# Uneven placement of the seven-product units in the mixer's weave

## The chip, the cores and the metric

The kernel runs on one core of a Trainium2 chip. The metric is the device time of one execution in microseconds (us). The kernel before takes 2188.45 us, the median of three runs that lie between 2188.09 and 2190.01 us.

## The reference

One encoder layer on x of 256 rows by 2048 columns, all in float32: a SwiGLU block with a norm, a mixer with a norm, a second SwiGLU block with a norm, and a gated per-layer embedding. The change touches the mixer:

```python
proj = x @ w_in
mq, mk, mv, mo, mi, mf, sq, sk, sv, ga, gb = _split_cols(proj)
...
y_m = (h.reshape(bsz, s, D_M) * jax.nn.sigmoid(mo)).astype(x.dtype)
y_sb = _stick_breaking(_heads(sq, N_HEADS_SB), _heads(sk, N_HEADS_SB), _heads(sv, N_HEADS_SB))
merged = jax.nn.sigmoid(ga) * (y_m @ w_up_m) + jax.nn.sigmoid(gb) * (y_sb @ w_up_sb)
return merged @ w_out
```

`h` is the output of a chunkwise mLSTM with 4 heads of 256; `y_sb` is stick-breaking attention with 8 heads of 128. `ga` and `gb` have 2048 columns each, `mo` has 1024.

## The kernel before

**Matmuls.** Each float32 operand is split into a high part that TensorE takes in its float32r format and a low part, the rest. A product needs three matmuls (L1259 to L1261: high by high, high by low, low by high). A *unit* (class `Unit`) is one weight tile of 256 rows by up to 512 columns, against one half of the 256 tokens: two steps of 128 rows, so six matmuls of up to 512 columns. A weight tile is loaded by DMA as `raw` (L1182, 512 KB), ScalarE casts its high half (L1210, `split`), VectorE subtracts to get the low half (L1214). `splits_due` keeps tiles split ahead of TensorE: the mode "wide" that holds during the weave allows 8 raw tiles and 6 split ones.

**Plain groups.** `group` makes pairs of units: one weight tile is used for both token halves. A pair therefore needs one split for two units.

**Seven-product units.** `seven` computes two column groups for two token halves as a two-by-two block product with seven products instead of eight (`both7` calls it for two column groups of `w_in`). It makes 28 units: four of product 1, four of product 2, then four rounds of products 5, 7, 6, 4, 3. Every unit has a weight tile of its own, and four of the seven tiles are sums of others, which VectorE makes with an addition in place (L361, `raw<-raw`). The finished products are combined by VectorE (L396 in `put`, L402 in `rest`) or copied by ScalarE (L412). Within the four rounds five PSUM banks stay in use at a time, beside the two of the plain group that runs at the same time; there are eight.

**Order.** All engines' instructions are written out in one pass over `program`, a list of units. Small steps of the attention branches (`mlstm`, `gated`, `stick`, `sb_turn`) are generators in a scheduler, `Sched`, whose clock goes on by 6 x 0.2161 us for each full unit; a step is written out when its due time on that clock has come, and each engine then runs its own instructions in the order written. PSUM tiles, `mm` for units and `ms` for small steps, share the eight banks. The matmuls of the small steps stand among those of the units: L705 (transposes after a projection), L867 and L881 (mLSTM), L916 (transposes of the gated mLSTM output, whose low half VectorE makes in L922), L935 (scores of stick-breaking attention), L948 and L949 (cumulative sums, which VectorE takes from PSUM in L950), L959 (attention by values). L833 and L944 are VectorE steps of the same attention.

**The weave.** In the mixer a stretch of the program mixes two lists (L1061 to L1063). `main` has 144 units in plain groups:

- `sb(10, 11, 4, 5)`, `sb(20, 21, 22, 23)`, `sb(12, 13, 6, 7)`: 16 units each; `sb(14, 15)`: 16 units with 256 columns only. They give the stick-breaking heads their inputs, and the chains of attention steps run beside them and beside the gate groups.
- `branch(0, 0)` and `branch(0, 1)`: 16 units each, the gates of column group 0. ScalarE takes their sigmoid straight from PSUM.
- `ups(0, True)`, `ups(1)`, `ups(2)`: 16 units each, the products with `w_up_m` and `w_up_sb`. VectorE multiplies each with its gate (L1019, L1021). Before `ups(0)` the mLSTM outputs that were written to DRAM are read back (`bring_ym_back`).

`side` has 4 x 28 seven-product units: the output gate `mo`, which the gated mLSTM steps wait for, then `pair(1)`, `pair(2)`, `pair(3)`, the gates of column groups 1 to 3, which `ups(1)`, `ups(2)` and, behind the weave, `ups(3)` need. `weave` puts side units behind main units, at an even rate.

Of the kernel before, what the change touches and what calls it, by code (L numbers as in the profile page):

```python
# [23 lines left out]
COL = 512  # L24
# [80 lines left out]
class ActT:  # L105
# [17 lines left out]
    def ready(self, c, tt):  # L123
        return self.left.get((c, tt)) == 0
# [35 lines left out]
        self.name = name  # L160


def weave(main, side):

    n = sum(isinstance(u, Unit) for u in main)
    out, at, seen = [], 0, 0
    for u in main:
        out.append(u)
        if isinstance(u, Unit):
            seen += 1  # L170
            while at < len(side) and at * n < seen * len(side):
                out.append(side[at])
                at += 1
    return out
# [11 lines left out]
def kernel(  # L186
# [9 lines left out]
    w_in, w_out, w_up_m, w_up_sb = w_in[0], w_out[0], w_up_m[0], w_up_sb[0]  # L196
# [194 lines left out]
    def both7(w, ca, cb, act, dest, ready, loaded):  # L391

        r, held = {}, {}

        def put(k, t, a, b, op):
            nc.vector.tensor_tensor(out=r[k, t], in0=a, in1=b, op=op)  # L396

        def rest():
            u = r[0, 1]
            put(0, 1, held[7], u, ALU.add)  # L400
            z = r[1, 1] = dest(1, 1)
            nc.vector.scalar_tensor_tensor(out=z, in0=u, scalar=-1.0, in1=held[5],  # L402
                                           op0=ALU.mult, op1=ALU.subtract)
            ready(1, 1)
            return
            yield

        def done(m, ps):
            held[m] = ps
            if m == 1:  # L410
                r[0, 1] = dest(0, 1)
                nc.scalar.copy(r[0, 1], ps)  # L412
            elif m == 2:
                r[0, 0] = dest(0, 0)
                put(0, 0, ps, r[0, 1], ALU.add)
                ready(0, 0)
            elif m == 6:
                r[1, 0] = dest(1, 0)
                put(0, 1, ps, r[0, 1], ALU.add)
                put(1, 0, held[5], r[0, 1], ALU.add)  # L420
                sched.spawn(rest(), DELAY["rest"])
            elif m == 4:
                sched.until(lambda: (1, 1) in r)
                put(0, 1, ps, r[0, 1], ALU.add)
                ready(0, 1)
            elif m == 3:
                put(1, 0, ps, r[1, 0], ALU.subtract)
                ready(1, 0)

        return seven(w, ca, w, cb, D, COL, act, done, loaded)  # L430

    program = []

    def mode(name):
        program.append(Mode(name))
# [105 lines left out]
    def ffn(w1, w3, w2, act, norm, skew=True, ahead=()):  # L541
# [74 lines left out]
        def down(*chunks):  # L616
            pairs = []
            for g in range(D // COL):
                def add(ps, t, g=g):
# [11 lines left out]
                    + down(6, 8, 7))  # L631
        side = [u for c in (1, 2, 3, 5, 6, 7, 9, 10) for u in up7(c)]
        program.extend(main[:HEAD] + weave(main[HEAD:], side))
        program.append(norm.load)
        program.extend(ahead)
# [13 lines left out]
    x1T = ActT(act_tile, ActT(act_tile), True)  # L649
# [334 lines left out]
    def sb(*heads):  # L984
        if heads[0] >= 16:
            col0 = sq0 + heads[0] * DS
        else:
            col0 = [(sq0 + h * DS, 2 * DS) for h in heads[::2]]
        return flat(group(w_in, range(0, D, 2 * P), col0, len(heads) * DS, x1T,
                          lambda ps, t: sb_columns(ps, t, heads)))  # L990
# [40 lines left out]
    def branch(g, half):  # L1031
        return flat(group(w_in, range(0, D, 2 * P), ga0 + half * D + g * COL, COL, x1T, gate_done(g, half)))

    def ups(g, swap=False):
        parts = [flat(group(w_up_m, range(0, HM * DM, 2 * P), g * COL, COL, ymT, up_done(g, 0, swap))),
                 flat(group(w_up_sb, range(0, HS * DS, 2 * P), g * COL, COL, ysbT, up_done(g, 1, not swap)))]
        if swap:
            parts.reverse()
        return parts[0] + parts[1]

    def gate_dest(g):
        def dest(k, t):
            if (g, t) not in gt:
                gt[g, t] = big()
            return gt[g, t][:, k * COL:(k + 1) * COL]
        return dest

    def gate_ready(g):
        def sigmoid(k, t):
            a = gt[g, t][:, k * COL:(k + 1) * COL]  # L1050
            activate(a, a, ACT.Sigmoid)
            flags.add(("gate", g, t, k))
            return
            yield
        return lambda k, t: sched.spawn(sigmoid(k, t), DELAY["sig"])

    def pair(g):
        return both7(w_in, ga0 + g * COL, ga0 + D + g * COL, x1T, gate_dest(g), gate_ready(g), False)

    program.append(sticks)  # L1060
    main = sb(10, 11, 4, 5) + sb(20, 21, 22, 23) + sb(12, 13, 6, 7) + sb(14, 15) + branch(0, 0) + branch(0, 1) + [bring_ym_back] + ups(0, True) + ups(1) + ups(2)  # L1061
    mode("wide")
    program.extend(weave(main, both7(w_in, 3072, 3072 + COL, x1T, mo_dest, mo_ready, False) + pair(1) + pair(2) + pair(3)))  # L1063
    mode("mix")
    program.append(bring_back)
    program.append(lambda: [sched.spawn(merge_turn(g, t), 1.0 + 2.0 * g + t) for g in range(3) for t in range(TT)])
# [69 lines left out]
    at = len(program) - 24  # L1136
# [160 lines left out]
```

## Time and profile before

| | |
|---|---|
| Median of three runs | 2188.45 us |
| The profiled execution | 2189.97 us |
| Its span, first to last instruction | 2188.3 us |
| TensorE busy | 2175.6 us |
| VectorE busy | 1902.8 us |
| ScalarE busy | 1316.0 us |
| Mean DMA rate | 260 GB/s |

In rows of the profile PE is TensorE's matmuls, PEld its weight loads, DVE is VectorE, ACT is ScalarE, POOL is GpSimd, SP is SyncE, which issues the DMAs. A row of instructions of one line shows the line, engine, operation, output<-inputs, shapes and the count, then the busy time in us, the mean of one in ns and, behind the second bar, the idle time of the engine before them with what ended it. A row of the waits shows who waited for whom, with the total in us, the number of waits and the longest. A row of stretches shows its length and each engine's busy time with its count of instructions, then the granted TensorE clock, the DMA engines' share and GB/s. A row of the timeline has the start and the duration in us; where it ends in xN it joins N instructions in a row, and a bracket gives the idle time before it. TensorE's matmuls overlap, so their durations are longer than the time from one start to the next.

### The profile page before, as it was taken

How to read it: one execution, taken by the hardware profiler on the slowest of the kernel's cores; microseconds unless marked ns; L12 is line 12 of the kernel's file. 1: busy time of each engine (PE TensorE's matmuls, PEld its weight loads, DVE VectorE, ACT ScalarE, POOL GpSimd, SP SyncE). 2: the span in 40 equal slices, each digit the busy share in tenths (PEclk: the TensorE clock that was granted, in tenths of full speed). 3: DMA queues.
4: the chain of work that ended last, by engine and by line, in shares of the span. 5: the costliest groups of instructions: out<-in, count | busy, mean ns of one | idle time of the engine just before them, and what ended most of it. 6: DMA issues, size and time to landing. Idle time of an engine off the chain costs nothing.

```text
span 2188.3 us, 28264 instructions
## 1 busy us (share of the span) xinstructions
PE 2175.6 (99%) x9966; PEld 1800.1 (82%) x9966; DVE 1902.8 (87%) x2108; ACT 1316.0 (60%) x1591; POOL 97.9 (4%) x88
## 2 busy tenths in 40 slices
PE   9999999999999999999999999999999999999999
PEld 7888888888887888888888888888888888888888
DVE  6999999899998765898988985699999999999974
ACT  7555655556564755667775554566665555665572
POOL 0100000010000000000000000000010000000000
PEclk9999999999999999999999999999999999999999
DMA  9899999899994775667878886589999999999753
GB/s 336 249 306 283 289 295 305 273 279 315 308 333 155 214 233 154 193 206 209 299 217 281 271 267 212 183 236 309 287 275 305 306 272 290 309 295 321 253 166 102
DMA packets 302222, 568.52 MB, mean 260 GB/s; under 512 B 18264, under 2 KB 39680, under 8 KB 302080
## 3 DMA queue, kind: packets, MB, share of 16 engines
q1 hardware_dynamic: 280320, 524.77, 71.8%
q0 software_dynamic: 21760, 41.95, 11.2%
q8 instruction: 78, 1.28, 0.2%
q14 instruction: 64, 0.52, 0.1%
HBM read 560.35 MB, written 6.29 MB: 259 GB/s over the span
## 4 chain that ended last, share of the span: by engine, by line
PE 92%; DMA 3%; DVE 3%; issue 1%; ACT 1%; POOL 0%; SPq 0%; DVEq 0%; POOLq 0%; ACTq 0%
PE mm L1261 29%; PE mm L1259 29%; PE mm L1260 29%; DMA raw<-in_ffn_w_dram 3%; DVE split L1214 2%; PE ms L290 1%; PE ms L495 0%; ACT split L1210 0%; DVE big L621 0%; DVE raw L361 0%; PE ms L959 0%; DMA raw<-in_w_in_dram 0%; PE ms L867 0%; PE ms L881 0%; PE ms L935 0%
## 5 line engine op out<-in xcount | busy, mean ns | idle before, releaser
L1210 ACT CAST split<-raw 128x1024 fp32r<-128x1024 f32 (+2 forms) x1061 | 1060.7, 1037 | 522.5 <-PE mm L1260 150.7
L1214 DVE TENSOR_TENSOR split<-raw,split 128x1024 fp32r<-128x1024 f32 (+2 forms) x1061 | 1240.7, 1200 | 137.0 <-ACT split L1210 119.1
L1259 PE MATMUL mm<-split,actT 128*128 128x512 f32 (+2 forms) x3120 | 1216.7, 390 | 0.1
L1261 PE MATMUL mm<-split,actT 128*128 128x512 f32 (+2 forms) x3120 | 1203.0, 386 | 3.3 <-DVE actT L297 3.3
L1260 PE MATMUL mm<-split,actT 128*128 128x512 f32 (+2 forms) x3120 | 1202.0, 385 | 1.8 <-DVE split L1214 1.7
L1261 PEld LDWEIGHTS mm<-split,actT 128*128 128x128 f32 x3120 | 586.1, 188 | 124.5 <-DVE actT L297 5.4
L1260 PEld LDWEIGHTS mm<-split,actT 128*128 128x128 f32 x3120 | 586.8, 188 | 117.0 <-DVE split L1214 4.8
L1259 PEld LDWEIGHTS mm<-split,actT 128*128 128x128 f32 x3120 | 586.5, 188 | 114.1 <-issue 1.3
L361 DVE TENSOR_TENSOR raw<-raw 128x1024 f32<-128x1024 f32 x240 | 292.5, 1219 | 2.2
L1187 POOL DMA_DIRECT2D raw<-in_ffn_w_dram x80 | 95.4, 1193 | 1879.9 <-DVE temp L559 786.3
L292 ACT CAST actT<-ms 128x512 fp32r<-128x512 f32 x60 | 35.0, 586 | 76.9 <-PE ms L290 75.8
L568 DVE TENSOR_TENSOR temp<-mm,temp 128x512 f32<-128x512 f32 x112 | 76.8, 685 | 4.2 <-PE mm L1261 1.9
L621 DVE SCALAR_TENSOR_TENSOR big<-mm,big 128x512 f32<-128x512 f32 x96 | 65.1, 682 | 7.3 <-PE mm L1261 7.2
L297 DVE TENSOR_TENSOR actT<-ms,actT 128x512 fp32r<-128x512 f32 x60 | 40.7, 683 | 17.4 <-ACT big L296 9.0
L236 ACT ACT_TABLE_LOAD x35 | 44.9, 1283 | 0.6
L285 DVE TENSOR_TENSOR actT<-temp,actT 128x512 fp32r<-128x512 f32 x40 | 26.5, 687 | 17.3 <-ACT actT L284 17.1
L240 ACT ACTIVATE temp<-mm 128x512 f32<-128x512 f32 (+1 forms) x22 | 12.3, 559 | 44.8 <-PE mm L1261 44.8
L240 ACT ACTIVATE temp<-temp 128x512 f32<-128x512 f32 (+1 forms) x48 | 28.5, 595 | 9.9 <-DVE temp L568 7.3
L284 ACT CAST actT<-temp 128x512 fp32r<-128x512 f32 x40 | 24.1, 621 | 13.0 <-DVE temp L308 12.1
L240 ACT ACTIVATE rstd<-mv,eps 128x1 f32<-128x1 f32 x6 | 1.8, 295 | 45.1 <-DVE mv L478 45.1
L1076 DVE SCALAR_TENSOR_TENSOR big<-big,mm 128x512 f32<-128x512 f32 x8 | 5.5, 685 | 26.9 <-PE mm L1261 26.9
L794 DVE SCALAR_TENSOR_TENSOR temp<-ms,cw,temp 128x253 f32<-128x253 f32 (+2 forms) x48 | 22.4, 480 | 7.3 <-ACT temp L240 6.1
(128 smaller groups left out, 561.2 us busy)
## 6 DMA issues: line engine op xcount, KB each, us to landing
raw<-in_ffn_w_dram SPq DMA_DIRECT2D x655, 512.0 KB, 6.3
raw<-in_w_in_dram SPq DMA_DIRECT2D x176, 512.0 KB, 4.6
raw<-in_ffn_w_dram POOLq DMA_DIRECT2D x80, 512.0 KB, 9.2
raw<-in_w_out_dram SPq DMA_DIRECT2D x32, 512.0 KB, 6.0
raw<-in_w_in_dram SPq DMA_DIRECT2D x56, 256.0 KB, 3.7
raw<-in_w_ple_gate_dram SPq DMA_DIRECT2D x24, 512.0 KB, 4.6
raw<-in_w_up_sb_dram SPq DMA_DIRECT2D x16, 512.0 KB, 4.5
raw<-in_w_up_m_dram SPq DMA_DIRECT2D x16, 512.0 KB, 5.3
```

The lines of the kernel that those rows point to most:

```text
L236: nc.scalar.preload_act_table_set(table[0])
L240: nc.scalar.activation(out, in_, func, **kw)
L297: nc.vector.tensor_tensor(out=dst[:, 1], in0=ps[:], in1=dst[:, 0], op=ALU.subtract)
L361: nc.vector.tensor_tensor(out=out.tile[:, :, :cols], in0=a.tile[:, :, :cols], in1=b.tile[:, :, :cols], op=ALU.add)
L568: nc.vector.tensor_tensor(out=out, in0=a, in1=b, op=op)
L621: nc.vector.scalar_tensor_tensor(out=xs, in0=ps, scalar=0.5, in1=xs, op0=ALU.mult, op1=ALU.add)
L1187: nc.gpsimd.dma_start(out=r.tile[:, :, :r.cols], in_=r.plus[0], accum_op=ALU.add)
L1210: nc.scalar.copy(hi[:, ks], r[:, ks])
L1214: nc.vector.tensor_tensor(out=lo[:, ks], in0=r[:, ks], in1=hi[:, ks], op=ALU.subtract)
L1259: nc.tensor.matmul(ps, hi, w[0][:, k, :u.cols], start=first, stop=False)
L1260: nc.tensor.matmul(ps, hi, w[1][:, k, :u.cols], start=False, stop=False)
L1261: nc.tensor.matmul(ps, lo, w[0][:, k, :u.cols], start=False, stop=last)
```

## The change

`weave` takes a third argument, `bends`, a list of points (share of the main units, share of the side units). Side units are placed along straight lines through (0, 0), the bends and (1, 1), where before they followed one straight line. The weave of the mixer passes two bends, (0.55, 0.51) and (0.8, 0.81). A call without bends, such as the ones in both feed-forward blocks, places its units as before.

```diff
-def weave(main, side):
+def weave(main, side, bends=()):
     n = sum(isinstance(u, Unit) for u in main)
+    points = [(0.0, 0.0), *bends, (1.0, 1.0)]
+    def due(f):
+        for (x0, y0), (x1, y1) in zip(points, points[1:]):
+            if f <= x1:
+                return len(side) * (y0 + (f - x0) * (y1 - y0) / (x1 - x0))
...
-            while at < len(side) and at * n < seen * len(side):
+            while at < len(side) and at < due(seen / n) - 1e-6:
...
     mode("wide")
-    program.extend(weave(main, both7(w_in, 3072, 3072 + COL, x1T, mo_dest, mo_ready, False) + pair(1) + pair(2) + pair(3)))
+    program.extend(weave(main, both7(w_in, 3072, 3072 + COL, x1T, mo_dest, mo_ready, False) + pair(1) + pair(2) + pair(3),
+                         [(0.55, 0.51), (0.8, 0.81)]))
```

Share 0.55 of the main units lies just before the end of `branch(0, 0)`, share 0.8 in `ups(1)`.

## The prediction

> **What bounds the kernel now.** I read the page first: engine shares, then the chain that ended last.
>
> ```profile
> span 2188.3 us, 28264 instructions
> PE 2175.6 (99%) x9966; PEld 1800.1 (82%) x9966; DVE 1902.8 (87%) x2108; ACT 1316.0 (60%) x1591; POOL 97.9 (4%) x88
> PE 92%; DMA 3%; DVE 3%; issue 1%; ACT 1%; POOL 0%; SPq 0%; DVEq 0%; POOLq 0%; ACTq 0%
> ```
>
> TensorE is busy 99% of the span and carries 92% of the chain. The change neither adds nor removes a matmul, so it can only move the time in which TensorE waits. Such time is small anywhere: 2188.3 - 2175.6 = 12.7 us in the whole program. To see the share of the woven stretch I located it by counting: 640 units of six matmuls are issued before it, so its first matmul starts at 910.9 us and the one after its last at 1275.0 us. I cut it where the main list changes: three full-width attention groups, the narrow group with half of the first gate group, the rest of the gates with the first half-group of `ups(0)`, the other half of `ups(0)`, then `ups(1)` and `ups(2)`.
>
> ```profile
> core 0: us, PE busy (x) PEld busy (x) DVE busy (x) ACT busy (x) POOL busy (x), PEclk, DMA share, GB/s
> 910.90:1040.30 129.40, 129.33 (x590) 106.33 (x589) 115.98 (x142) 94.68 (x131) 0.00 (x0) 1.00 0.69 206
> 1040.30:1094.20 53.90, 52.84 (x290) 44.89 (x289) 53.28 (x64) 38.79 (x60) 0.00 (x0) 1.00 0.90 301
> 1094.20:1178.00 83.80, 83.59 (x375) 68.94 (x374) 72.04 (x76) 58.34 (x73) 0.00 (x0) 1.00 0.75 237
> 1178.00:1200.00 22.00, 21.94 (x97) 17.79 (x96) 19.16 (x22) 15.00 (x16) 0.00 (x0) 1.00 0.91 288
> 1200.00:1275.00 75.00, 75.00 (x333) 62.10 (x332) 74.30 (x73) 43.06 (x45) 0.00 (x0) 1.00 0.82 266
> ```
>
> VectorE is full in two stretches, 53.28 of 53.90 us beside the narrow group and 74.30 of 75.00 us in the last two `ups`, and has 83.80 - 72.04 = 11.8 us free between them. TensorE idles in the weave only 129.40 - 129.33 + 1.06 + 0.21 + 0.06 = 1.4 us, three quarters of it in the narrow stretch. The waits of TensorE and of VectorE inside the weave say for what:
>
> ```profile
> PE ms L705 <- DVE temp L950: 0.7, 1, 0.7
> PE ms L935 <- DVE actT L922: 0.4, 1, 0.4
> PE ms L959 <- DVE temp L950: 0.2, 1, 0.2
> DVE split L1214 <- ACT split L1210: 23.0, 23, 3.2
> ```
>
> No weight half is late in a way that shows here; the three waits are attention and transpose steps that need a result, or a PSUM bank, which VectorE releases late.
>
> **The change part by part.** *What moves.* The side list holds 4 x 28 = 112 seven-product units, the main list 144. Before, after main unit s, ceil(112 s / 144) side units have been placed. After, the share runs through (0.55, 0.51) and (0.8, 0.81). Counting both: at main unit 48, where the narrow group begins, 35 are placed and not 38; at 64, where it ends, 47 and not 50; at 76, 55 and not 60; at 104 both 81; at 112 both 88; at 117, 93 and not 91, then 0 or 1 ahead to the end. So at most five units move later, and one or two are early in `ups(1)` and `ups(2)`. The order of instructions is the same outside the weave. The counts are equal on TensorE, VectorE, POOL and the DMA queue; ScalarE loses two activation-table loads.
>
> *What one unit costs.* From the groups inside the weave:
>
> ```profile
> L1214 DVE TENSOR_TENSOR split<-raw,split 128x1024 fp32r<-128x1024 f32 (+1 forms) x183 | 214.7, 1195 | 26.0 <-ACT split L1210 23.0 <-PE mm L1260 2.3
> L361 DVE TENSOR_TENSOR raw<-raw 128x1024 f32<-128x1024 f32 x64 | 77.9, 1218 | 0.3
> L396 DVE TENSOR_TENSOR big<-mm,big 128x512 f32<-128x512 f32 x23 | 15.7, 684 | 0.1
> L236 ACT ACT_TABLE_LOAD x15 | 19.2, 1283 | 0.2
> ```
>
> On TensorE a unit takes 6 x 75.00/333 = 1.35 us (last stretch). On VectorE a side unit needs one split (1.195), 64/112 of a weight addition (0.696) and 28/112 of a 0.684 us eviction (0.171): 2.06 us, or 0.71 us more than TensorE gives it. A main unit shares its split with the other token half, 0.60 us, and so pays back 0.75 us. Placing side units later is thus a loan: each one not yet placed leaves VectorE 0.71 us further ahead, and it is repaid when the unit comes.
>
> *The relief.* In the narrow group VectorE stands 3 x 0.71 = 2.1 us better, by main unit 76 it stands 5 x 0.71 = 3.6 us better. What that meets there:
>
> ```profile
> 1076.45 1.22 DVE L1214 TENSOR_TENSOR split<-raw,split 128x1024 fp32r<-128x1024 f32 x1
> 1079.18 0.39 PE L1260 MATMUL mm<-split,actT 128*128 128x512 f32 x1
> 1078.72 3.49 DVE L1214 TENSOR_TENSOR split<-raw,split 128x1024 fp32r<-128x1024 f32 x3
> 1082.13 0.55 DVE L944 SCALAR_TENSOR_TENSOR temp<-temp 128x384 f32<-128x384 f32 x1
> 1082.71 0.43 DVE L833 TENSOR_TENSOR temp<-temp,bound 128x256 f32<-128x256 f32 x1
> 1083.05 1.22 DVE L1214 TENSOR_TENSOR split<-raw,split 128x1024 fp32r<-128x1024 f32 x1
> 1084.19 0.55 DVE L950 TENSOR_TENSOR temp<-temp,ms 128x384 f32<-128x384 f32 x1
> 1083.71 0.39 PE L1261 MATMUL mm<-split,actT 128*128 128x512 f32 x1
> 1084.79 0.44 PE L705 MATMUL ms<-ident,temp 128*128 128x128 f32 x2 [0.70 <-DVE temp L950]
> ```
>
> The low half that ends at 1077.67 is first read at 1079.18 (pairing the k-th split with the k-th weight): 1.5 us of lead. The transposes of L705 wait for L950, which has been queued behind splits back to back since 1078.72. L1261 to L705 takes 1.08 us where a matmul lasts 0.23, so 0.85 us are lost. With VectorE some 3 us earlier L950 runs about 1081, before L705 is due: I take all of the 0.85. The wait of L935 has the same cause:
>
> ```profile
> 1065.49 0.39 PE L1261 MATMUL mm<-split,actT 128*128 128x512 f32 x1
> 1066.24 0.81 PE L935 MATMUL ms<-big 128*128 128x256 f32 x3 [0.36 <-DVE actT L922]
> 1143.36 0.39 PE L1261 MATMUL mm<-split,actT 128*128 128x512 f32 x1
> 1143.96 0.78 PE L959 MATMUL ms<-temp,big 128*128 128x256 f32 x3 [0.21 <-DVE temp L950]
> ```
>
> 0.75 - 0.23 = 0.52 us; 2 us of relief cover it, and I take it too. The third loses 0.60 - 0.23 = 0.37 us in the middle stretch, where relief is being repaid; I leave it. Bounds of the gain: 0 (each of these steps finds another VectorE instruction ahead of it) to 0.85 + 0.52 + 0.37 = 1.74 us; taken: 1.37.
>
> *The repayment.* Between main units 72 and 104 the changed order places 81 - 52 = 29 side units against 25: 4 x 0.71 = 2.8 us more VectorE than TensorE time, against 11.8 us free. That hides it, with one doubt: the free time is mostly waiting for ScalarE's cast (23.0 us over the weave), so not all of it can be used. Then comes the saturated stretch:
>
> ```profile
> 1245.12 1.22 DVE L1214 TENSOR_TENSOR split<-raw,split 128x1024 fp32r<-128x1024 f32 x1
> 1248.02 0.39 PE L1260 MATMUL mm<-split,actT 128*128 128x512 f32 x1
> ```
>
> Here the low half is ready 1.7 us before its use (1246.34 to 1248.02). At the same place the changed order has placed as many side units as before, so it starts from the same debt; but in `ups(1)` one or two units are early, 0.7 to 1.4 us of lead spent sooner. Bounds: nothing (1.7 us of lead covers it) to 1.4 us, if the lead is already gone from the middle. A main group also changes four times there, and a VectorE eviction that runs later can keep the bank of the next group. I take 0.4 us, near the lower end, because the trace shows no wait of TensorE at all in that stretch.
>
> *Covered parts.* The two table loads save 2 x 1.283 us on ScalarE, which has 75.00 - 43.06 us free in the last stretch and 15 us in the narrow one: nothing. Weight loads move with their units: a side unit needs 6 loads for 7 units, a main unit one for two, so the middle (main units 72 to 104) goes from 16 + 21.4 loads in 57 units to 16 + 24.9 in 61, 2% more a unit. That raises its 237 GB/s to about 242, below the 301 of the narrow stretch: nothing; a load later than that would be a late cast. The output gate `mo` is complete after main unit 38 instead of 35, some 3 units or 4 us later, so the mLSTM's gated steps and their trip to DRAM shift by that, and are read back only before `ups(0)`, at main unit 96: nothing, unless a write were still under way there.
>
> *Sum.* -0.85 - 0.52 + 0.4 = -1.0 us. The profiled execution took 2189.97 us, 1.7 around its span of 2188.3, so it would become 2189.0; it is 1.5 us above the median of the runs, 2188.45, and against that the forecast is 2187.4.
>
> **The rivals.** *The debt falls due in the last `ups` (slower).* Suppose the middle's free time can't be used, because VectorE there waits for ScalarE's cast and not for work. Then the repaid 5 x 0.71 = 3.6 us stay missing when `ups(1)` begins, and VectorE, 99% busy from 1200 us on, can't win them back. Of the 1.7 us of lead nothing is left and TensorE waits 3.6 - 1.7 = 1.9 us for splits, plus 1.4 for the early units: +3.3 - 1.37 = +1.9, or 2190.4; with the gains missing too, 2191.8. It decides once the lead at 1200 us is over 1.7 us shorter than before. For it: 23.0 us of VectorE's waits are for ScalarE. Against: only about 3 of the 11.8 us are needed, and casts move together with their splits.
>
> *The same in one piece (slower still).* If the missing 3.3 us came as one gap, TensorE might resume at a lower pace. The trace has that pace only at the start, where the same shape of matmul takes longer than in the weave:
>
> ```profile
> L1147 PE MATMUL ms<-ones 128*128 128x128 f32 x14 | 3.6, 433 | 1.1 <-DVE ones L244 1.1
> L949 PE MATMUL ms<-temp,ones 128*128 128x128 f32 x16 | 3.1, 274 | 0.0
> ```
>
> 14 x 159 ns = 2.2 us, so 2190.4 + 2.2 = 2192.6. For it: VectorE does work in runs of several splits. Against: splits come one by one, a late one costs at most its own 1.2 us at a time, and the granted clock was 1.00 in every stretch above, the 0.70 us wait included. The Trainium skill, "TensorE: Matmul & The Clock Gate" (section "HAM oscillation — how this bites in real kernels"), warns of TensorE gaps over about 3.4 us, after which the clock is halved. No run here shows such a gap; by an estimate from that page this rival would cost 3.4/2 = 1.7 us where the rows give 2.2.
>
> *The wait only changes its place (no change).* The PSUM banks are handed on in order and the chains' steps come at intervals fixed by a model clock, so each step removed from a busy moment meets another: 2188.4. For it: all three waits sit on these steps. Against: in the changed order they meet a VectorE with fewer splits queued.
>
> *All three waits go, and nothing is repaid (faster).* 2188.45 - 1.74 = 2186.7. More can't be had in this stretch.
>
> That the change doesn't do what it says is excluded: the changed order of instructions shows the counts above.
>
> **How the numbers follow.** Forecast (2187.4, within 0.8) 43%; wait moved 18%; debt due 17%; in one piece 3%; all gone 12%; a stall that I have not found, over 4.4 us, 7%. A difference under 0.2% (4.4 us) can hardly be told from no change. Faster by that needs more than all waits of the weave: 2%, out of the 12. Slower by it needs about 2192.8, beyond the debt's 2191.8: the 3% in one piece, which lies at that border, and the 7%. Within: 88%. Range 2186.2 (all gone, and half a microsecond of the runs' spread of 1.9) to 2191.3 (most of the debt).
>
> **What would show it.** Right: L705 and L935 no longer among TensorE's waits, VectorE under 97% beside the narrow group and above 86% (72.04 of 83.80) between 1094 and 1178 us, and no TensorE wait over 0.5 us from 1178 on. Wrong: waits of TensorE for L1214 or L1019 after 1178 us; new waits on L867 to L965 of more than 1.4 us together; or a granted clock below 1.00.

## The result and the profile after

The changed kernel takes 2192.79 us, the median of 22 runs (2189.72 to 2195.91), against 2188.12 us (2185.99 to 2190.13) for the kernel before in as many runs beside it: 4.7 us more, ratio 1.0021 with a 95% interval of 1.0015 to 1.0027. The forecast was 1 us less, and the range ended at 2191.3.

In the rows of the changed kernel the line numbers are higher by 7, from L1071 on by 8: L705 is L712 now, L916 L923, L922 L929, L935 L942, L361 L368, L950 L957, L959 L966, L1019 L1026, L1214 L1222, and the three matmuls of a unit are L1267 to L1269. First the page's head:

```profile
span 2190.7 us, 28258 instructions
PE 2176.2 (99%) x9966; PEld 1800.6 (82%) x9966; DVE 1903.9 (87%) x2108; ACT 1313.7 (60%) x1589; POOL 97.9 (4%) x88
```

TensorE is busy nearly as long as before (2176.2 against 2175.6 us), so what was added is mostly waiting. The weave, cut at the same main units as before (0, 48, 72, 104, 112, 144), shows where:

```profile
core 0: us, PE busy (x) PEld busy (x) DVE busy (x) ACT busy (x) POOL busy (x), PEclk, DMA share, GB/s
911.29:1035.93 124.64, 124.64 (x570) 102.78 (x569) 109.26 (x132) 87.90 (x124) 0.00 (x0) 1.00 0.67 201
1035.93:1091.88 55.95, 52.00 (x286) 43.91 (x284) 53.44 (x64) 40.10 (x61) 0.00 (x0) 1.00 0.87 278
1091.88:1180.83 88.95, 88.95 (x402) 73.59 (x401) 77.95 (x85) 62.16 (x77) 0.00 (x0) 1.00 0.77 248
1180.83:1201.22 20.39, 20.39 (x91) 16.89 (x90) 18.03 (x20) 12.82 (x15) 0.00 (x0) 1.00 0.90 294
1201.22:1278.85 77.63, 76.80 (x337) 62.91 (x336) 77.36 (x77) 44.76 (x46) 0.00 (x0) 1.00 0.82 263
sum 367.56, PE 362.78 PEld 300.08 DVE 336.05 ACT 247.74 POOL 0.00; mean PE 72.56 PEld 60.02 DVE 67.21 ACT 49.55 POOL 0.00
```

The weave lasts 367.56 us against 364.1. TensorE idles 3.95 us beside the narrow group (before 1.06) and 0.83 us in `ups(1)` and `ups(2)` (before none). Outside the weave the two profiled executions differ by -1.1 us, which is no more than such executions of one kernel differ. TensorE's waits inside the weave:

```profile
PE ms L712 <- DVE actT L929: 2.0, 1, 2.0
PE ms L923 <- DVE actT L929: 1.1, 1, 1.1
PE ms L942 <- DVE actT L929: 0.9, 1, 0.9
PE mm L1267 <- DVE big L1026: 0.8, 2, 0.4
```

The waits for L950 (now L957) are gone. In their place three small steps wait for L929, which makes the low half of a gated mLSTM transpose and is the last reader of its PSUM bank: a gated transpose behind the one before it (L923), a score step (L942, which is L935 of before and waited for the same line there) and a transpose of the narrow group (L712). The longest, from the timelines of VectorE, TensorE and ScalarE:

```profile
1070.82 0.38 PE L923 MATMUL ms<-ident,big 128*128 128x128 f32 x2
1069.86 2.35 DVE L1222 TENSOR_TENSOR split<-raw,split 128x1024 fp32r<-128x1024 f32 x2
1072.13 0.55 DVE L951 SCALAR_TENSOR_TENSOR temp<-temp 128x384 f32<-128x384 f32 x1
1072.71 0.42 DVE L840 TENSOR_TENSOR temp<-temp,bound 128x256 f32<-128x256 f32 x1
1072.94 0.61 ACT L247 ACTIVATE actT<-ms,cw 128x128 fp32r<-128x128 f32 x2
1073.06 2.35 DVE L1222 TENSOR_TENSOR split<-raw,split 128x1024 fp32r<-128x1024 f32 x2
1075.33 0.60 DVE L929 SCALAR_TENSOR_TENSOR actT<-ms,cw,actT 128x128 fp32r<-128x128 f32 x2
1075.98 0.33 PE L712 MATMUL ms<-ident,temp 128*128 128x128 f32 x1 [2.00 <-DVE actT L929]
```

The gated transposes (L923) take 0.2 us at 1070.8, but their bank is held until 1075.9. ScalarE reads it first and is done at 1073.55; L929 needs that result, and then still stands behind two splits, the last of the six VectorE instructions ahead of it. The next small step, L712, needs that bank: it is 2.0 us late and starts 5.2 us behind the gated transposes.

### The profile page after: what moved, and what is told of

It reads as the page before. It is cut to its first block, busy times and chain, and to the rows that moved or that the text cites. A ratio compares the mean times of both kernels' runs of the same rounds, so it can differ in the third digit from the quotient of the medians.

```text
span 2190.7 us, 28258 instructions
## 1 busy us (share of the span) xinstructions
PE 2176.2 (99%) x9966; PEld 1800.6 (82%) x9966; DVE 1903.9 (87%) x2108; ACT 1313.7 (60%) x1589; POOL 97.9 (4%) x88
## 4 chain that ended last, share of the span: by engine, by line
PE 92%; DVE 4%; issue 1%; DMA 1%; ACT 1%; SPq 0%; DVEq 0%; ACTq 0%; POOLq 0%
PE mm L1269 30%; PE mm L1267 30%; PE mm L1268 30%; DVE split L1222 2%; PE ms L297 1%; DVE raw L368 1%; DMA raw<-in_ffn_w_dram 0%; PE ms L502 0%; ACT split L1218 0%; DVE big L628 0%; DMA temp<-in_ln_g_dram 0%; PE ms L942 0%; PE ms L874 0%; PE ms L966 0%; PE ms L888 0%
## 5 line engine op out<-in xcount | busy, mean ns | idle before, releaser
L1222 DVE TENSOR_TENSOR split<-raw,split 128x1024 fp32r<-128x1024 f32 (+2 forms) x1061 | 1242.1, 1203 | 131.9 <-ACT split L1218 115.6
L1267 PE MATMUL mm<-split,actT 128*128 128x512 f32 (+2 forms) x3120 | 1217.0, 390 | 0.8 <-DVE big L1026 0.8
L1269 PE MATMUL mm<-split,actT 128*128 128x512 f32 (+2 forms) x3120 | 1203.4, 386 | 2.9 <-DVE actT L304 2.9
L1269 PEld LDWEIGHTS mm<-split,actT 128*128 128x128 f32 x3120 | 586.2, 188 | 123.9 <-DVE actT L304 5.1
L1267 PEld LDWEIGHTS mm<-split,actT 128*128 128x128 f32 x3120 | 586.7, 188 | 115.4 <-DVE big L1026 1.7
L368 DVE TENSOR_TENSOR raw<-raw 128x1024 f32<-128x1024 f32 x240 | 293.0, 1221 | 2.2
```

Of the source, the lines that this page charges most:

```text
L368: nc.vector.tensor_tensor(out=out.tile[:, :, :cols], in0=a.tile[:, :, :cols], in1=b.tile[:, :, :cols], op=ALU.add)
L1222: nc.vector.tensor_tensor(out=lo[:, ks], in0=r[:, ks], in1=hi[:, ks], op=ALU.subtract)
L1267: nc.tensor.matmul(ps, hi, w[0][:, k, :u.cols], start=first, stop=False)
L1269: nc.tensor.matmul(ps, lo, w[0][:, k, :u.cols], start=False, stop=last)
```

## The experiments

The theories, once the result was known. **A:** with `mo` complete about 3 units later, the gated transposes fall among the transposes of the narrow group; both use the one PSUM bank that seven open accumulators leave. **B:** the thinner placement itself costs VectorE its lead. **C**, a closer form of A: how long the bank is held depends on VectorE's queue. The expectations count for a wait what TensorE loses from one start to the next, less the time of a matmul (4.4 us behind L929, 1.2 us for L1026); the rows and the text give its idle time alone (4.0 and 0.8 us). Times stand against runs of the kernel before on the same chip: 2188.36 us in the first four experiments, 2188.91 in the next four, 2189.06 in the last four. The changed kernel stands 4.7 us above its own.

**`mo` kept in place.** Edit to the changed kernel:

```diff
-                         [(0.55, 0.51), (0.8, 0.81)]))
+                         [(0.25, 0.25), (0.55, 0.51), (0.8, 0.81)]))
```

> The changed kernel with one more bend, (0.25, 0.25), so that the 28 units of mo stand where they stood before, and only later side units are thinned out. Theory A (mo complete later puts the gated mLSTM transposes among the transposes of the narrow attention group, one spare PSUM bank for both; 4.4 us of new TensorE waits at 1060 to 1076 us): those three waits shrink to under 1.5 us together and the time falls to about 1 to 1.5 us above before. Rival B (the thinner placement itself costs VectorE its lead, since it idles at its limit of split tiles before the narrow group and is then short in it): waits of 3 to 5 us stay in the narrow group and the time stays about 4.5 us above before.

2190.17 us, ratio 1.0008 (0.9999 to 1.0017). The waits:

```profile
PE ms L966 <- DVE temp L957: 1.2, 1, 1.2
PE mm L1267 <- DVE big L1026: 0.9, 2, 0.5
PE ms L942 <- DVE actT L929: 0.8, 1, 0.8
```

Of 4.0 us behind L929, 0.8 are left, and the time is 1.8 above before, a little over A's 1.5; a step of the attention chain has a wait of its own now. This speaks for A, but the edit also leaves ten side units in the narrow group where the changed kernel has twelve.

**The sigmoid of `mo` sooner.**

```diff
     def mo_ready(k, t):
...
-        sched.spawn(sigmoid(), DELAY["sig"])
+        sched.spawn(sigmoid(), 0.0)
```

> The changed kernel, all side units as in it, but the sigmoid of mo is due at once and not 5 us of the model clock later, so that the gated mLSTM transposes come some 3 to 7 units earlier, about where they stood before. Theory A: the three waits for the low half of the gated output vanish (under 1.5 us together) and the time falls by 3 to 4 us to about 1 to 1.5 us above before. Rival B: as many side units beside the chains as in the changed kernel, so the same 4.4 us of waits, on other steps, and no change of the time.

2193.45 us, ratio 1.0022 (1.0013 to 1.0032): a miss for A as I had put it. The gated transposes did come 4 to 9 units sooner, but waits of 2.1 us behind L929 were left, now on L942 twice, and another of 2.4 us appeared at 964 us, on L712 for L957. Moving one chain alone didn't clear the bank: its steps met others instead. Since the sigmoid moves too, this run can't tell A from B.

**Only the first bend, only the second.** The two added lines belong to one run each:

```diff
-                         [(0.55, 0.51), (0.8, 0.81)]))
+                         [(0.55, 0.51), (0.8, 0.8)]))
...
+                         [(0.55, 0.55), (0.8, 0.81)]))
```

> Only the first bend acts: (0.55, 0.51), then (0.8, 0.8), so the units in ups(1) and ups(2) are on the old line again. Both theories: the waits at 1060 to 1076 us stay (4 to 5 us), since placement up to main unit 79 is the same. If the one or two early units of the second bend cause the two waits for the eviction by the gates at 1242 and 1262 us (1.2 us together), these go and the time is about 1.2 us under the changed kernel; if VectorE's missing lead at 1200 us (2.9 us instead of 4.2) causes them, they stay at 0.5 to 1.5 us.

> Only the second bend acts: (0.55, 0.55), then (0.8, 0.81). Everything up to main unit 79 is as before. Both theories of the narrow group: no wait for the gated low half beyond the 0.5 us of before, and the two waits of before (0.85 and 0.52 us) are back. If the second bend alone costs the waits for the eviction by the gates, 0.5 to 1.2 us of them show from 1178 us on and the time is 0.5 to 1.2 us above before; otherwise it is within 0.5 us of before.

The first bend alone takes 2191.90 us (1.0016, 1.0007 to 1.0025), the second alone 2188.76 (1.0001, 0.9992 to 1.0009). With the first alone the three waits behind L929 are all there (2.0, 1.1 and 0.8 us) and those for L1026 are gone; with the second alone the two waits of before are back and one of 0.4 us for L1026 appears. So the first bend costs 3.5 us, and the second 0.4 us, which the interval doesn't tell from nothing. The early units in `ups(1)` and `ups(2)` cause the waits for the gate evictions, since these come and go with the second bend.

**Only the gated steps later.** The kernel before, its placement untouched:

```diff
-        due = max(sched.now, st.get("gated", 0.0))
+        due = max(sched.now + (0.0 if "gated" in st else 5.0), st.get("gated", 0.0))
```

> The kernel before, its even placement of side units untouched; only the first gated mLSTM step waits 5 us longer on the model clock, so that its transposes come about 4 us later, as they do in the changed kernel. Theory A (the later gated steps alone cause the waits in the narrow group, since they then stand close to other steps that need the one spare PSUM bank): 2.5 to 5 us of TensorE waits between 1050 and 1090 us in place of the 1.4 us of before, and the time 1.5 to 4 us above before. Rival B (VectorE's lead, spent by the changed placement, is the cause): waits and time within 1 us of before.

2191.77 us, ratio 1.0016 (1.0007 to 1.0025), 2.9 us above before, as A has it. In the rows of this kernel the line numbers are those of before:

```profile
PE ms L959 <- DVE temp L950: 1.7, 1, 1.7
PE ms L916 <- DVE actT L922: 1.6, 1, 1.6
PE ms L935 <- DVE actT L922: 0.9, 1, 0.9
PE ms L705 <- DVE temp L950: 0.3, 1, 0.3
```

No side unit has moved, and the waits for L922 are 2.5 us, where they were 0.4. B isn't needed for that: a 5 us shift of one chain suffices. The gated transposes come 4 to 11 units later here, in the changed kernel 3 to 9. The wait of L959 shows that the later steps of the attention chains move as well, since all of them ask for bank slots on one list.

**Less work for VectorE.** The changed kernel without the weight additions of `pair(1)`:

```diff
             def make():
-                nc.vector.tensor_tensor(...)
+                if ca != ga0 + COL:
+                    nc.vector.tensor_tensor(...)
```

> The changed kernel without the 16 weight additions of pair(1), which stand beside and behind the narrow group; the gates of column group 1 are then not those of the reference. Every TensorE instruction keeps its place; VectorE has 16 x 1.22 = 19.5 us less to do between about 1036 and 1100 us. Theory C (a bank is held until VectorE gets to the low half, behind the splits queued ahead of it; how long depends on VectorE's backlog): the three waits for the gated low half fall from 4.4 us to under 1 us together, and the time to 2188 to 2189 us. If the waits come from the order of the steps alone, whatever VectorE's backlog, 3 us or more of them stay.

2188.97 us, ratio 1.0000 (0.9991 to 1.0010): C's time. Of 4.0 us behind the gated low half 1.4 stay (0.9 and 0.5), more than the 1 us that C allowed: with VectorE relieved the bank is free sooner, but not always in time.

**ScalarE alone reads the bank.** The changed kernel and, as a control, the kernel before:

```diff
+            full = hs[:, t].rearrange("q (b s) -> q b s", s=P)
             for d, src, g in parts:
                 activate(d[:, 0], src, ACT.Copy, scale=g)
-            for d, src, g in parts:
-                nc.vector.scalar_tensor_tensor(out=d[:, 1], in0=src, scalar=g, in1=d[:, 0], op0=ALU.mult, op1=ALU.subtract)
+            for k, (d, src, g) in enumerate(parts):
+                activate(full[:, k], src, ACT.Copy, scale=g)
+            for k, (d, src, g) in enumerate(parts):
+                nc.vector.tensor_tensor(out=d[:, 1], in0=full[:, k], in1=d[:, 0], op=ALU.subtract)
```

> The changed kernel, with the gated low half taken in another way: ScalarE writes the scaled transpose to SBUF as well (16 more casts of 0.36 us), and VectorE subtracts from there, so that ScalarE alone reads the PSUM bank and releases it. Side units and the order on TensorE are those of the changed kernel. Theory C: the waits for the gated low half (4.4 us) shrink to under 1.5 us, now for ScalarE, and the time falls by 3 to 4 us to 2189 to 2190 us; the two waits at the gate evictions (1.2 us) stay. Rival: ScalarE is as late as VectorE in the narrow group, and the time stays within 1 us of the changed kernel.

> The kernel before with the same other way for the gated low half. Theory C: of its 2.0 us of TensorE waits in the weave only the 0.5 us behind the gated low half go, the other two (0.85 and 0.37 us, behind the cumulative sum) stay; the time is 0 to 0.7 us under before. A control for the price of the 16 added casts: if they cost time by themselves, it lies above before.

The changed kernel comes down to 2189.53 us (1.0003, 0.9994 to 1.0012), 0.6 above before where it was 4.7 above, so about 4 us less, with every TensorE instruction in its place:

```profile
PE ms L712 <- ACT big L247: 1.8, 1, 1.8
PE mm L1270 <- DVE big L1029: 0.9, 2, 0.5
```

Two of the three waits are gone; the third stays, now for ScalarE. The control takes 2189.15 (1.0002, 0.9993 to 1.0010): the edit gains nothing there. The wait of L935 stays at 0.4 us, for ScalarE, which I had expected to vanish, and L705 waits 1.4 us and not 0.7. So it isn't the edit by itself that is worth about 4 us, but what it undoes of the change.

**The second bend off as well.** The changed kernel with the bank edit above, and with (0.55, 0.51), (0.8, 0.8) in the weave.

> The changed kernel without its second bend and with ScalarE alone reading the bank of the gated transposes, the two edits that took 0.9 and 3.3 us off it each by itself. If the two costs are separate, they add up: the waits for the gate evictions fall under 0.3 us, one wait for ScalarE of about 2 us stays at 1073 us, and the time is 4 to 4.5 us under the changed kernel, 2188.3 to 2189 us, so no faster than before.

2189.65 us, ratio 1.0000 (0.9991 to 1.0009): 0.6 us above before, as with the bank edit alone, though the waits for the evictions are gone as expected. The two costs don't show as a sum; the second one, 0.4 to 0.9 us in the other runs, is of the size of what eleven runs can tell.

**Thinned inside the narrow group only.**

```diff
-                         [(0.55, 0.51), (0.8, 0.81)]))
+                         [(1 / 3, 1 / 3), (4 / 9, 0.415), (5 / 9, 5 / 9)]))
```

> Bends (1/3, 1/3), (4/9, 0.415), (5/9, 5/9): as before up to main unit 48, three side units fewer inside the narrow group (38 to 47 and not 38 to 50), made up by main unit 80, then as before. mo stands where it stood before. If thinning relieves VectorE where it is full, as my prediction had it (3 x 0.71 = 2.1 us), the two waits of before at 1065 and 1084 us (1.4 us) fall under 0.5 us and the time is 0.5 to 1.4 us under before. If the order of the steps at the spare bank decides (the narrow group passes sooner, and a gated step now comes at unit 112, just ahead of the transposes at 114), waits of 1 us or more for the gated low half appear and the time is at or above before.

2189.09 us, ratio 0.9999 (0.9990 to 1.0008). The two waits of before are gone, as the relief would have it, and one of 1.6 us for L929 has come, on L712: the order at the bank takes back what the relief gives.

**Seven split tiles.** The changed kernel:

```diff
-HELD = {"ffn": (8, 6), "mix": (5, 6), "wide": (8, 6)}
+HELD = {"ffn": (8, 6), "mix": (5, 6), "wide": (6, 7)}
```

> The changed kernel with seven split tiles and six raw ones during the weave in place of six and eight; the order on TensorE is unchanged. If VectorE's lead is capped by the six split tiles, so that the thinner placement ahead of the narrow group only makes it idle, its lead there rises by about one unit, 1.2 to 1.4 us, the waits for the gated low half fall from 4.4 to 2.5 to 4 us, and the time by 0.5 to 2 us. But steps of VectorE that come later in the same queue then stand behind one more split; if that weighs more, or six raw tiles are too few, the waits stay at 4.4 us or rise, and the time is at or above the changed kernel.

2194.42 us, ratio 1.0023 (1.0014 to 1.0032), 5.4 above before. VectorE does gain lead: the low half of the first weight of the narrow group is ready 8.67 us before its first use, in the changed kernel 6.98 (pairing the k-th split with the k-th weight). More lead doesn't help, which speaks against B; the wait of L942 grows from 0.9 to 2.1 us. That it grows because each VectorE step now stands behind one more split is argued, not shown: the raw tiles are fewer as well. Part of the time is the clock (last section): the three executions with a mean granted clock of 1.000 have a median of 2192.6 us, the seven with 0.999 one of 2195.5.

**The other way round.**

```diff
-                         [(0.55, 0.51), (0.8, 0.81)]))
+                         [(1 / 3, 0.36), (4 / 9, 0.43), (5 / 9, 5 / 9)]))
```

> The other way round: bends (1/3, 0.36), (4/9, 0.43), (5/9, 5/9), so that two to three side units come earlier ahead of the narrow group, where VectorE has free time, and it has two fewer inside; from main unit 80 as before. mo is complete sooner and the gated steps end about 4 units sooner, ahead of the transposes of the narrow group. Theory A: no wait for the gated low half over 0.5 us, TensorE waits in the weave 0.5 to 2 us together, the time between 1 us under before and the same. Rival: the weave ahead of the narrow group has no room for them, waits for splits or chain steps before 1040 us of 1 to 3 us, the time 1 us or more above before.

2186.94 us (2184.69 to 2191.92), ratio 0.9991 (0.9982 to 1.0000): 2.1 us under before, at the edge of what the runs can tell. Its weave, cut at about the same places:

```profile
910.44:1038.10 127.66, 127.66 (x585) 105.19 (x584) 116.36 (x141) 93.10 (x128) 0.00 (x0) 1.00 0.67 213
1038.10:1094.20 56.10, 56.10 (x305) 48.12 (x304) 53.89 (x65) 43.97 (x66) 0.00 (x0) 1.00 0.87 287
1094.20:1178.00 83.80, 83.80 (x377) 69.14 (x375) 72.95 (x78) 60.52 (x75) 0.00 (x0) 1.00 0.73 242
1178.00:1200.00 22.00, 21.94 (x97) 18.04 (x97) 20.26 (x24) 13.30 (x15) 0.00 (x0) 1.00 0.91 292
1200.00:1272.20 72.20, 72.20 (x320) 59.77 (x319) 71.54 (x70) 42.48 (x43) 0.00 (x0) 1.00 0.81 262
sum 361.76, PE 361.70 PEld 300.26 DVE 334.99 ACT 253.37 POOL 0.00; mean PE 72.34 PEld 60.05 DVE 67.00 ACT 50.67 POOL 0.00
```

TensorE idles 361.76 - 361.70 = 0.06 us in the whole weave, though VectorE is nearly as full beside the narrow group as it was: 2.2 us idle of 56.10. In the order written, the last gated transposes stand at unit 101 of the weave, in the changed kernel at 112; the narrow group's own stand at 117 and 119, there at 114 and 116. VectorE's lead at the first weight of the narrow group is smaller than in the changed kernel, 4.05 us against 6.98, so it isn't lead that removed the waits. That the order did agrees with A, but the run also thins the group, so it doesn't show it alone. The weave is 2.3 us shorter than before and 5.8 shorter than in the changed kernel.

## Why the prediction was wrong

**What bounds the kernel: right.** TensorE's busy time is nearly unchanged, and what moved is waiting for VectorE, most of it at small steps. In the weave it idles 4.8 us and not 1.4. Over the thirteen kernels other than the one before, the time moves with this idle time to within 1.3 us.

**The step that failed: the covered parts.** I costed the later `mo` at nothing: "so the mLSTM's gated steps and their trip to DRAM shift by that, and are read back only before `ups(0)`, at main unit 96: nothing". I looked at who reads the gated output, not at what its making holds on the way: a PSUM bank, for which other steps queue. The gated transposes also moved by 3 to 9 units and not by 3, since their slots are handed out on one list with those of the other steps. Shifted alone in the kernel before, the gated steps cost 2.9 us; the bank released by ScalarE gave about 4 us back. The case stood beside my rivals ("the wait only changes its place"), but that rival assumed the new waits to be as long as the old ones. They were 4.0 us against 1.1 beside the narrow group. Two of my signs of being wrong came: 1.1 us of waits on L916 and 0.5 us more on L935 are over the 1.4 us that I allowed, and there are waits for L1019 after 1178 us.

**The relief: wrong as a loan, right at the place.** "Each one not yet placed leaves VectorE 0.71 us further ahead" holds only while VectorE may run ahead. Before the narrow group it idled 129.40 - 115.98 = 13.4 us before, and 124.64 - 109.26 = 15.4 in the changed kernel: the 2.0 us that I had lent are idle time, not lead. The low half of the group's first weight is ready 7.07 us before its use in the kernel before and 6.98 in the changed one; that a seventh split tile makes it 8.67 shows that six tiles were the limit. Inside the group VectorE's work was the same, twelve side units and 53.44 us against 53.28. My sign of the relief, VectorE under 97% there, came true all the same (53.44 of 55.95 us), because the new waits made the stretch longer. Thinning only inside the group did lower VectorE's load (51.87 of 54.40 us) and removed both old waits (1.37 us by my count). That agrees with how I read them; since the edit also moves the steps, it doesn't show it alone.

**The waits of L705 and L935.** I took 1.37 us off for them. Both steps wait still: L705 2.0 us and for another instruction, L929 where it was L950; L935 0.9 us and for the same one, L922 (now L929). "2 us of relief cover it" was wrong for it. That a step is late for one thing says nothing of what it is late for next.

**The repayment: mechanism right, size off.** I took 0.4 us with 1.4 as the upper bound; the two waits for the gate evictions come to 0.8 us, and each bend tried alone shows that the second causes them. No wait for a split appeared.

**The slower rivals.** "The debt falls due in the last `ups`" was wrong in its effect: the lead at the start of `ups(1)` did shrink, from 4.4 to 3.2 us, but TensorE never waited for splits. The form "in one piece" priced a lower pace at 2.2 us and tied it to that place. The clock did go down, by an estimate at a cost of 1.7 us, but beside the narrow group and in the run with seven split tiles (last section); the profiled execution of the changed kernel shows no such stretch in the weave. The range ended 1.5 us too low: its upper end came from the debt, and no term stood for a bank that is held.

**Still open.** The profiled weave is 3.5 us longer, the medians are 4.7 apart. In 12 of the 22 runs of the changed kernel the mean granted clock is 0.999 and not 1.000, against 3 of 31 runs of the kernel before in the first set of experiments. The 12 have a median of 2192.9, the other 10 of 2192.2. But with the first bend alone and with the sooner sigmoid the runs with 0.999 are the shorter ones, by 1.0 and 0.7 us, so what the clock adds to the changed kernel's time isn't shown.

## What to carry to other kernels

Where two lists of work are woven, moving one also moves every chain that waits for it. Before costing such a shift at nothing, list what the shifted steps hold (a PSUM bank, a queue place) and who asks for it next, and compare the step spacing with the time until the last reader gets to it. A lead that is bounded by a ring of buffers can't be saved up: thin work out where the engine is full, and put the excess where it idles at the bound, as the last experiment did.

## What the runs showed of the hardware

The kernel with seven split tiles shows the clock going down in the middle of a dense stretch. Its timeline and stretches:

```profile
1072.59 0.39 PE L1269 MATMUL mm<-split,actT 128*128 128x512 f32 x1
1075.03 0.69 PE L712 MATMUL ms<-ident,temp 128*128 128x128 f32 x2 [2.05 <-DVE actT L929]
1075.94 0.63 PE L1268 MATMUL mm<-split,actT 128*128 128x512 f32 x1
1076.37 0.63 PE L1269 MATMUL mm<-split,actT 128*128 128x512 f32 x1
```

```profile
1071.53:1074.94 3.41, 1.44 (x7) 0.86 (x5) 3.41 (x6) 1.57 (x4) 0.00 (x0) 1.00 0.87 281
1074.95:1078.35 3.40, 3.32 (x9) 2.75 (x10) 3.40 (x4) 1.32 (x2) 0.00 (x0) 0.50 1.04 408
1078.36:1081.77 3.41, 3.41 (x17) 2.76 (x17) 1.64 (x3) 1.76 (x3) 0.00 (x0) 1.00 0.77 263
```

At the end of a wait of 2.05 us the granted clock falls to 0.50, for 3.41 us. Two matmuls start 0.43 us apart there where 0.23 is usual, and 9 run in that time where the next stretch has 17. By an estimate, half of the 3.41 us is lost on top of the wait, 1.7 us. The weave of this run is 6.5 us longer than before, and only 4.6 us of that are waiting.

The length of a wait doesn't decide alone. The changed kernel's 2.00 us, 2.02 us with the first bend alone, 2.12 us at 1063.5 us in this same run, and 2.37 us with the sooner sigmoid left the clock at 1.00. The traces suggest what does. In all 14 of them each stretch of full clock lasts a whole multiple of 3.4133 us (637, 638 or 639 times, here 312 and 327), so the clock changes on a grid of that step. In the step before the fall TensorE idles 3.41 - 1.44 = 1.97 us. The other four waits were cut by a border of the grid, into 1.21 and 0.79 us, 1.09 and 0.93, 1.19 and 0.93, 1.36 and 1.01. From the start of full clock on, every step with 1.97 us or more of idle time is followed by 0.50, this one and those at the end of each program, where TensorE has nothing left to do; no step with 1.81 us or less is.

The grid starts at another moment in each execution: full clock begins 8.4 us after the first instruction in the trace of the kernel before, 10.2 us in that of the changed one. So the same wait may or may not bring the clock down. The runs agree: of the four kernels whose longest wait in the weave is 2.0 us or more, 30 of 52 executions have a mean granted clock under 1.000, of the other nine changed ones 7 of 98, of the kernel before 7 of 96. The low clock at the program's end alone brings the mean to 0.9995 in the trace of the kernel before, so a few may come from there.

The Trainium skill, "TensorE: Matmul & The Clock Gate" (section "HAM oscillation — how this bites in real kernels"), warns of gaps over about 3.4 us. This case doesn't agree: 2.05 us sufficed in one execution, and the measurement decides. A wait of 2 us on TensorE can already cost more than its length.
